# Where the weight sums of the last feed-forward stand: three of sixteen steps moved out of the recurrence's and the attention's parts

## The chip, the cores and the metric

The kernel runs on one core of a Trainium2 chip. A core has a matrix engine (TensorE, PE in the profile, with its weight loads as PEld), a vector engine (VectorE, DVE), a scalar engine (ScalarE, ACT), a general engine (GpSimd, POOL), and a queue engine that here issues transfers only (SyncE, SP). Each engine executes its own instructions strictly in order; semaphores order them between engines. Sixteen DMA engines, shared by all queues, move data between the main memory and SBUF. The metric is the device time of one execution in microseconds.

## The reference

One residual block of a streaming encoder, on x of 256 rows and 1024 columns in fp32: a half-weight SwiGLU feed-forward; a mixer with two branches; a cross attention to a memory of 256 rows; a second SwiGLU feed-forward.

```python
h = rmsnorm(x, ffn1_pre_g);  x = x + 0.5 * rmsnorm(swiglu(h, ffn1_w_in, ffn1_w_down), ffn1_post_g)
h = rmsnorm(x, mix_pre_g)
q_a, f_a, i_a, g_a, q_b, k_b, v_b, f_b, gates = split(h @ w_in)
o_a = rmsnorm(hgrn2_chunkwise(q_a, f_a, i_a, lb), hg_norm_g) * silu(g_a)   # gated linear recurrence, 8 heads of 128
o_b = fox_attention(q_b, k_b, v_b, f_b + fox_f_bias)                       # causal softmax with summed log forget gates
gate = sigmoid(gates + b_gate)
y = gate[0] * (o_a @ w_branch_a) + gate[1] * (o_b @ w_branch_b)
x = x + rmsnorm(y @ w_out, mix_post_g)
x = x + rmsnorm(mem_cross_attention(rmsnorm(x), rmsnorm(mem), w_mq, w_mkv, w_mo), mem_post_g)   # 4 heads of 256
h = rmsnorm(x, ffn2_pre_g);  x = x + 0.5 * rmsnorm(swiglu(h, ffn2_w_in, ffn2_w_down), ffn2_post_g)
```

## The kernel before

**Products.** Every large product is made to nearly fp32 accuracy from fp32r parts: an operand is split into a high part `hi` and a rest `lo`, and three matmuls (hi by hT, lo by hT, hi by lT) stand for one. Weights come from the main memory in pieces of 512 KB (`raw`, four buffers, issued on SP, L136). ACT casts a piece to `hi` (L137), DVE subtracts to get `lo` (L138); `hi` and `lo` have eight buffers each. A chunk of a projection is four pieces. Activations are split in the same way (`hT` by ACT, `lT` by DVE: L156 and L157, L271 and L272 with a gain, L1240 and L1241 for the memory's values). PSUM has buffers `mm` (2), `tr` (2) and `acc` (4). A product group of a projection that has its features on the partitions is 48 matmuls 256 wide into one `mm`. All matmuls go through one helper (L93); the scores of the attention and the inner products of the recurrence are plain fp32.

**Stages in order of time.** Feed-forward 1; the mixer's projections: input (`i_a`), forget gates (`f_a`, whose last products DVE takes up at 235 us), queries (`q_a`), output gates and forget logits; then the k and q of the attention (`k_b`, `q_b`), among which the recurrence is laid in pieces; from 345 us the attention with the values' projection (`v_b`), into which the transposes of the recurrence's output are laid (to 380); the branch gates (`gates`), the branches, `w_out`; the memory stage (`mk`, `mq`, `mv`), whose softmax is transposed at 565; feed-forward 2.

**The steps.** Feed-forward 2 computes four pairs of its chunks (3, 5, 7, 9: `QUADS_2`) with fewer products, from sums of weights. These sums are made beforehand, in 16 steps spread over the program. A step is `at(name, c)`: if `(name, c)` stands in the table `SUMS_AT`, four additions run on DVE over a 1 MB tile `wide` (L771 to L774, 128x512 each), then two transfers on POOL's queue write the result to the main memory (`sums<-wide`, L776), then `load_step()` loads the data of a later step by two transfers on POOL's queue (`wide<-in_wts_dram`, L759). The place of the call in the program, and `issue_after` the last DVE instruction recorded, set where the additions stand on DVE. Step number k in the table takes the k-th slot of weights; so when an entry is taken out, all later entries change their slot.

`wide` has two buffers: the load for step k+2 goes into the buffer of step k, so it waits until the writes of step k have landed. POOL's queue is in order: while its first instruction waits, everything behind it waits too, the masks of the attention among it. Up to the branch gates only `TO_GATES` slots are loaded, since one buffer of `wide` is then lent to the gates' bias (`brow`, L1115).

**The attention's start.** `cbc` and `cbm` are the summed log forget gates, spread over the partitions by transfers on POOL's queue (L1017, L1021); on `cbm` POOL lays the causal mask (`affine_select`, L1023). `cc` is transposed into a `tr` buffer and copied to `ct` by DVE (L1030). Two groups of diagonal scores go into `tr` buffers, two wide groups into `acc` buffers; these hold the recurrence's last sums until DVE has multiplied them into `G` (L1013), for which the reciprocal root `rstd` is worked out by a chain of one-column operations on DVE (`v`, `y`, `t`: L223 to L239). Then `G` is transposed by PE (L315) and split into `hT` and `lT`.

**The memory's softmax.** Scores in `acc`; row maxima on DVE (L1258), exponentials on ACT (L1262), division on DVE (`pm`, L1264), transposes on PE (L1268).

**What sets the order.** The program is recorded with a few numbers that place parts behind a given matmul (`after`); a scheduler then lays each engine's instructions out. So a step taken out can change the order of its neighbours.

Of the kernel before, what the change touches and what calls it, by code (L numbers as in the profile page):

```python
# [53 lines left out]
L_MX = 30  # L54

SUMS_AT = (
    ("i_a", 1), ("f_a", 0), ("f_a", 1), ("q_a", 0), ("k_b", 1), ("v_b", 1), ("gates", 1), ("gates", 3),
    ("br_a", 0), ("br_b", 0), ("br_a", 1), ("br_b", 1), ("mk", 1), ("mk", 3), ("mq", 1), ("mv", 1),
)
TO_GATES = 6  # L60
L_LAST = 12

_ORDER = [
# [15 lines left out]
def block_kernel(ctx: ExitStack, tc: tile.TileContext, wts, head_in, gf_in, x_in, mem_in, memT_in, cols, rows, fbias, masks, out):  # L79
# [23 lines left out]
    def nm(s):  # L103
        count[0] += 1
        return f"{s}_{count[0]}"

    def m4(shape, dt=F32, n="m"):
        return mp.tile(shape, dt, tag="m4", name=nm(n))
# [38 lines left out]
    def chunk(name, c):  # L147
        return [unit(name, 4 * c + i) for i in range(4)]
# [46 lines left out]
    def proj_col2(X, units, cbs):  # L195
        ps = mm()
        for j, cb in enumerate(cbs):
            proj_col(ps[:, j * T : (j + 1) * T], X, units, cb)
        return ps.rearrange("p (c t) -> p c t", c=2)

    def bc(a, shape, dim):
        return a.unsqueeze(dim).to_broadcast(shape)
# [546 lines left out]
    def load_step():  # L749
        if len(slots) < len(steps) and (brows or len(slots) < TO_GATES):  # L750
            c, q, i = steps[len(slots)]
            W = wp.tile([P, 2, 2, 512], F32, tag="wide", name=nm("wide"), bufs=2)
            for e in range(2):
                part, src = W[:, e].rearrange("p j n -> p (j n)"), wts[_AT["f2_in"] + 4 * (c + e - 1) + 2 * q + i]
                if len(slots) < 2:
                    with tc.issue_after(loads[-1]):
                        nc.sync.dma_start(part, src)
                else:
                    G.dma_start(part, src)  # L759
            slots.append(W)  # L760

    def at(name, c=0):

        if (name, c) not in SUMS_AT:
            return
        k = SUMS_AT.index((name, c))
        (u, q, i), W = steps[k], slots[k]
        last = next(x for x in reversed(nc.cur_bb.bb.instructions) if x.engine == mybir.EngineType.DVE)
        t1, t4, t3, t2 = (W[:, a, b] for a in range(2) for b in range(2))
        with tc.issue_after(last):  # L770
            V.tensor_tensor(out=t1, in0=t1, in1=t3, op=ALU.add)  # L771
            V.tensor_tensor(out=t3, in0=t3, in1=t2, op=ALU.add)
            V.tensor_tensor(out=t2, in0=t1, in1=t2, op=ALU.add)  # L773
            V.tensor_tensor(out=t4, in0=t2, in1=t4, op=ALU.add)  # L774
        for e in range(2):
            G.dma_start(sums[u][2 * e : 2 * e + 2, q, :, i * 512 : i * 512 + 512].rearrange("k p n -> p k n"), W[:, e])  # L776
        load_step()
# [33 lines left out]
    for c in range(2):  # L811
        u = chunk("f_a", c)
        f, k = m4([P, 4, T], n="f"), m4([P, 4, T], n="k")
        for j in range(2):
            js = slice(2 * j, 2 * j + 2)
            ps = proj_col2(X2, u, (2 * j, 2 * j + 1))
            f_last = V.tensor_tensor(out=f[:, js], in0=ps, in1=bc(row2, [P, 2, T], 1), op=ALU.mult).ins
            S.activation(f[:, js], f[:, js], AF.Sigmoid)
            for i in (2 * j, 2 * j + 1):
                hd = 4 * c + i  # L820
                V.tensor_scalar(out=f[:, i], in0=f[:, i], scalar1=olb[:, hd : hd + 1], scalar2=lbv[:, hd : hd + 1], op0=ALU.mult, op1=ALU.add)
        V.tensor_scalar(out=k, in0=f, scalar1=-1.0, scalar2=1.0, op0=ALU.mult, op1=ALU.add)
        fT.append(f)
        kT_.append(k)
        at("f_a", c)
    for c in range(2):
        u = chunk("q_a", c)
        q = m4([P, 4, T], n="q")
        for j in range(2):
            js = slice(2 * j, 2 * j + 2)  # L830
            ps = proj_col2(X2, u, (2 * j, 2 * j + 1))
            z = sp.tile([P, 2, T], F32, tag="z2", name=nm("z2"), bufs=3)
            V.tensor_tensor(out=z, in0=ps, in1=bc(row2, [P, 2, T], 1), op=ALU.mult)
            S.activation(q[:, js], z, AF.Sigmoid)
            V.tensor_tensor(out=q[:, js], in0=q[:, js], in1=z, op=ALU.mult)
        qT_.append(q)
        at("q_a", c)

# [133 lines left out]
    for c in range(2):  # L974
        for name, lst, sc in (("k_b", kb_, 1.0), ("q_b", qb_, 1.0 / math.sqrt(128.0))):
            u = chunk(name, c)
            t = m4([P, 4, T], n=name)
            m = len(log)
            for j in range(2):
                ps = proj_col2(X2, u, (2 * j, 2 * j + 1))  # L980
                for i in range(2):
                    V.scalar_tensor_tensor(out=t[:, 2 * j + i], in0=ps[:, i], scalar=sc, in1=row2, op0=ALU.mult, op1=ALU.mult)
            lst.append(t)
            at(name, c)
            if c == 0 and name == "k_b":
                forget(m + 30)

# [107 lines left out]
    for c in range(2):  # L1095
        u = chunk("v_b", c)
        t = m4([P, 2, 512], n="v_b")
        for h in range(2):
            ps = mm()
            proj_tok(ps, X2, u, h)  # L1100
            S.activation(t[:, h, :], ps, AF.Copy, scale=r2[h])
        vb_.append(t)
        at("v_b", c)
    for h in range(2):
        with after(len(log) - L_OA * (2 - h)):
            to_T(OA, lambda kb: Gt[h][:, kb * P : (kb + 1) * P], h, G_HG)
# [89 lines left out]
    for h in range(2):  # L1196
        rows_proj(po[h], Y, "w_out", h, range(0, 4))
        if h == 0:
            y_T(1, 1, m + L_Y)
    at("w_out", 0)  # L1200
    rowm = row_of(rm)
    rows_proj(po[0], Y, "w_out", 0, range(4, 8))
    post(po[0], 0, g2)
# [69 lines left out]
    def mem_out(i):  # L1273
        ps = trp()
        for j in range(2):
            o = ps[:, j * T : (j + 1) * T]
            for sb in range(2):

                n = sb * 512 + (2 * (i % 2) + j) * P
                vh = VM.h[i // 2][:, n // T, n % T : n % T + P]  # L1280
                vl = VM.l[i // 2][:, n // T, n % T : n % T + P]
                MM(o, vh, pT.h[sb][:, i], start=(sb == 0), stop=False)
                MM(o, vl, pT.h[sb][:, i], start=False, stop=False)
                MM(o, vh, pT.l[sb][:, i], start=False, stop=(sb == 1))
        i2 = slice(2 * (i % 2), 2 * (i % 2) + 2)
        split(AO.h[i // 2][:, i2], AO.l[i // 2][:, i2], ps.rearrange("p (a t) -> p a t", a=2))

    at("mv", 0)
    m = len(log)
    mem_v(1)  # L1290
    at("mv", 1)
# [2 lines left out]
            mem_out(i)  # L1294
    for i in range(2, 4):
        mem_out(i)
    X4 = Pair()
    r4 = [None, None]
    po = [[acc(), acc()], [acc(), acc()]]
# [7 lines left out]
    rows_proj(po[1], AO, "mo", 1, range(3, KB))  # L1307
    half(X4, r4, 0, G_F2, m + L_MO)
    post(po[1], 1, g3)


    def second(m):
        half(X4, r4, 1, G_F2, m + L_F2)

    ffn("f2_in", "f2_dn", X4, r4, 2, 3, QUADS_2, sums, None, second)

# [84 lines left out]
```

## Time and profile before

| | us |
|---|---|
| median of 3 runs (lowest, highest) | 789.82 (789.19, 791.26) |
| the profiled execution | 789.21 |
| its span on the core | 787.1 |
| PE busy in it | 775.7 (99%) |
| VectorE, ScalarE, GpSimd busy | 646.0, 469.5, 48.6 |

A row of an engine's timeline reads: start in us from the span's begin, duration in us, engine, line of the kernel, operation, output <- inputs, shapes, and xN for N like instructions in a row; in brackets the time for which the engine stood idle just before and what ended it. Matmuls are pipelined, so that the distance of their starts says more than their durations. "Chain" rows (the chain of work that ended last) have start, length, and the work or the wait. A fp32 product by PE shows as two records.

### The profile page before, as it was taken

The page shows a single profiled execution, that of the slowest core. Times are in us where ns is not written, and L with a number is a line of the kernel's source. Part 1 is how long each engine was busy: PE and PEld are TensorE (multiplying, and loading weights), DVE is VectorE, ACT ScalarE, POOL GpSimd, SP SyncE. Part 2 cuts the span into 40 slices and gives each one's busy share as a digit, 9 for nine tenths or more (in the row PEclk, how much of TensorE's full clock was granted, in tenths as well). Part 3 has the DMA queues.
Part 4 walks back from the last instruction along what each step waited for, and adds up shares of the span by engine and source line. Part 5 has one row for each costly group of instructions (what it writes and reads, how often), then busy time and mean ns, then how long its engine had stood idle before and what let it go on. Part 6 is the DMA issues. An engine that isn't in the chain of part 4 may idle for free.

```text
span 787.1 us, 13170 instructions
## 1 busy us (share of the span) xinstructions
PE 775.7 (99%) x5004; PEld 670.5 (85%) x5004; DVE 646.0 (82%) x1004; ACT 469.5 (60%) x704; POOL 48.6 (6%) x81
## 2 busy tenths in 40 slices
PE   9999999999999999999999999999999999999996
PEld 7888888887899999988788888999888888888884
DVE  6789989968788898689677886997777989888864
ACT  7665664756753447347675434745655758777753
POOL 0000000000102100030001221011000000000000
PEclk9999999999999999999999999999999999999998
DMA  9794484476679855584589999679664279889831
GB/s 346 247 311 159 160 294 148 160 248 244 252 258 311 277 189 162 178 293 132 192 286 327 376 355 359 210 259 334 231 200 148 84 262 374 315 312 344 321 126 54
DMA packets 57392, 193.61 MB, mean 246 GB/s; under 512 B 6249, under 2 KB 9713, under 8 KB 57329
## 3 DMA queue, kind: packets, MB, share of 16 engines
q1 hardware_dynamic: 48080, 159.60, 58.0%
q0 software_dynamic: 9104, 33.04, 12.0%
q8 instruction: 39, 0.64, 0.3%
q14 instruction: 25, 0.20, 0.1%
q10 hardware_dynamic: 144, 0.13, 0.0%
HBM read 174.92 MB, written 17.83 MB: 245 GB/s over the span
## 4 chain that ended last, share of the span: by engine, by line
PE 96%; DVE 1%; DMA 1%; ACT 1%; issue 1%; DVEq 0%; ACTq 0%
PE mm L93 62%; PE acc L93 27%; PE tr L93 4%; PE tr L395 1%; DMA raw<-in_wts_dram 1%; PE tr L315 1%; PE tr L1069 0%; ACT hi L137 0%; PE tr L1161 0%; PE tr L1268 0%; DVE lo L138 0%; ACT L357 0%; DVE y L229 0%; DVE t L227 0%; PE tr L406 0%
## 5 line engine op out<-in xcount | busy, mean ns | idle before, releaser
L138 DVE TENSOR_TENSOR lo<-raw,hi 128x1024 fp32r<-128x1024 f32 (+1 forms) x228 | 270.3, 1201 | 59.6 <-ACT hi L137 55.7
L137 ACT CAST hi<-raw 128x1024 fp32r<-128x1024 f32 (+1 forms) x228 | 232.4, 1036 | 120.5 <-PE mm L93 69.6
L93 PE MATMUL mm<-lo,hT 128*128 128x512 f32 (+1 forms) x448 | 171.2, 386 | 0.0
L93 PE MATMUL mm<-hi,hT 128*128 128x512 f32 (+1 forms) x448 | 170.7, 385 | 0.0
L93 PE MATMUL mm<-hi,lT 128*128 128x512 f32 (+1 forms) x448 | 170.6, 385 | 0.0
L93 PE MATMUL acc<-hi,act 128*128 128x512 f32 x352 | 113.2, 391 | 0.0
L93 PE MATMUL mm<-hT,hi 128*128 128x256 f32 x384 | 109.1, 284 | 0.1
L93 PE MATMUL mm<-hT,lo 128*128 128x256 f32 x384 | 109.0, 284 | 0.0
L93 PE MATMUL mm<-lT,hi 128*128 128x256 f32 x384 | 108.9, 284 | 0.0
L93 PEld LDWEIGHTS mm<-hi,hT 128*128 128x128 f32 x448 | 84.2, 188 | 16.1 <-ACT hT L271 0.7
L93 PEld LDWEIGHTS mm<-hi,lT 128*128 128x128 f32 x448 | 84.1, 188 | 15.8 <-DVE lT L272 0.5
L93 PEld LDWEIGHTS mm<-lo,hT 128*128 128x128 f32 x448 | 84.0, 188 | 14.8
L93 PEld LDWEIGHTS acc<-hi,act 128*128 128x128 f32 x352 | 65.9, 188 | 13.7 <-DVE act L157 0.2
L93 PEld LDWEIGHTS mm<-hT,hi 128*128 128x128 f32 x384 | 73.6, 192 | 0.5 <-issue 0.3
L93 PEld LDWEIGHTS mm<-hT,lo 128*128 128x128 f32 x384 | 73.6, 192 | 0.1
L93 PEld LDWEIGHTS mm<-lT,hi 128*128 128x128 f32 x384 | 73.6, 192 | 0.1
L93 PE MATMUL acc<-lo,act 128*128 128x512 f32 x176 | 69.0, 392 | 0.0
L157 DVE TENSOR_TENSOR lo<-wide,hi 128x1024 fp32r<-128x1024 f32 x40 | 48.0, 1219 | 2.0 <-ACT hi L156 1.4
L156 ACT CAST hi<-wide 128x1024 fp32r<-128x1024 f32 x40 | 41.5, 1051 | 12.3 <-DVE wide L494 7.5
L776 POOL DMA_DIRECT2D sums<-wide x32 | 23.6, 738 | 394.8 <-DVE wide L773 238.1
L93 PEld LDWEIGHTS acc<-lo,act 128*128 128x128 f32 x176 | 33.1, 188 | 6.7
L93 PE MATMUL mm<-hi,sh 128*128 128x512 f32 x96 | 37.5, 390 | 0.0
(243 smaller groups left out, 1130.2 us busy)
## 6 DMA issues: line engine op xcount, KB each, us to landing
raw<-in_wts_dram SPq DMA_DIRECT2D x232, 512.0 KB, 5.2
sums<-wide POOLq DMA_DIRECT2D x32, 512.0 KB, 5.8
wide<-sums SPq DMA_DIRECT2D x32, 512.0 KB, 6.8
wide<-in_wts_dram POOLq DMA_DIRECT2D x28, 512.0 KB, 6.6
wide<-in_wts_dram SPq DMA_DIRECT2D x12, 512.0 KB, 6.3
raw<-in_gf_dram SPq DMA_DIRECT2D x12, 344.0 KB, 4.7
head<-in_head_dram SPq DMA_DIRECT2D x8, 388.0 KB, 6.2
grow<-in_rows_dram SPq DMA_DIRECT2D x4, 512.0 KB, 6.9
```

Source lines behind the costliest of these rows:

```text
L93: log.append(PE.matmul(*args, **kw).ins)
L137: S.copy(h, r)
L138: V.tensor_tensor(out=l, in0=r, in1=h.bitcast(F32), op=ALU.subtract)
L156: S.copy(hi, src)
L157: V.tensor_tensor(out=lo, in0=src, in1=hi.bitcast(F32), op=ALU.subtract)
L315: PE.transpose(ps[:, j * P : (j + 1) * P], src(kb), ident)
L395: PE.transpose(trv[:, j, h * P : (h + 1) * P], ats[c, h][:, j * P : (j + 1) * P], ident)
L776: G.dma_start(sums[u][2 * e : 2 * e + 2, q, :, i * 512 : i * 512 + 512].rearrange("k p n -> p k n"), W[:, e])
```

## The change

Three steps leave their places (behind the first query chunk of the recurrence `q_a` 0, the second key and query chunk `k_b` 1, the second value chunk `v_b` 1). The call among the forget gates moves into the inner loop, so there are four places instead of two there; the table names three of them. The entries `mq` 0 (behind the memory's first query chunk) and `ao` 0 (a new call behind the memory's outputs) are new. `TO_GATES` goes from 6 to 4: two slots fewer are loaded ahead of the branch gates. Calls that no entry names any more are taken out.

```diff
 SUMS_AT = (
-    ("i_a", 1), ("f_a", 0), ("f_a", 1), ("q_a", 0), ("k_b", 1), ("v_b", 1), ("gates", 1), ("gates", 3),
-    ("br_a", 0), ("br_b", 0), ("br_a", 1), ("br_b", 1), ("mk", 1), ("mk", 3), ("mq", 1), ("mv", 1),
+    ("i_a", 1), ("f_a", 0), ("f_a", 2), ("f_a", 3), ("gates", 1), ("gates", 3), ("br_a", 0), ("br_b", 0),
+    ("br_a", 1), ("br_b", 1), ("mk", 1), ("mk", 3), ("mq", 0), ("mq", 1), ("mv", 1), ("ao", 0),
 )
-TO_GATES = 6
+TO_GATES = 4
...
@@ -819,10 +819,10 @@
             for i in (2 * j, 2 * j + 1):
                 hd = 4 * c + i
                 V.tensor_scalar(out=f[:, i], in0=f[:, i], scalar1=olb[:, hd : hd + 1], scalar2=lbv[:, hd : hd + 1], op0=ALU.mult, op1=ALU.add)
+            at("f_a", 2 * c + j)
         V.tensor_scalar(out=k, in0=f, scalar1=-1.0, scalar2=1.0, op0=ALU.mult, op1=ALU.add)
         fT.append(f)
         kT_.append(k)
-        at("f_a", c)
...
-        at("q_a", c)
...
-            at(name, c)
...
-        at("v_b", c)
...
-    at("w_out", 0)
...
-    at("mv", 0)
...
     for i in range(2, 4):
         mem_out(i)
+    at("ao", 0)
```

VectorE at the attention's start, before. The rows of lines 771 to 773 are additions of the step behind `v_b` 1; `ct` is the copy that frees a `tr` buffer.

```order
L223 TENSOR_SCALAR v_3901<-ss_666_3898 128x1
L138 TENSOR_TENSOR lo_4158<-raw_4156,hi_4157 128x1024
L225 TENSOR_SCALAR y_3903<-v_3901 128x1
L771 TENSOR_TENSOR wide_2432<-wide_2432 128x512
L227 TENSOR_SCALAR t_3905<-v_3901,y_3903 128x1
L772 TENSOR_TENSOR wide_2432<-wide_2432 128x512
L229 TENSOR_SCALAR y_3907<-t_3905,y_3903 128x1
L1030 COPY ct_3970<-tr_3971 128x16
L231 TENSOR_SCALAR t_3909<-v_3901,y_3907 128x1
L773 TENSOR_TENSOR wide_2432<-wide_2432 128x512
```

The same place now (the lines have moved up by two):

```order
L223 TENSOR_SCALAR v_3889<-ss_664_3886 128x1
L138 TENSOR_TENSOR lo_4146<-raw_4144,hi_4145 128x1024
L225 TENSOR_SCALAR y_3891<-v_3889 128x1
L227 TENSOR_SCALAR t_3893<-v_3889,y_3891 128x1
L229 TENSOR_SCALAR y_3895<-t_3893,y_3891 128x1
L231 TENSOR_SCALAR t_3897<-v_3889,y_3895 128x1
L233 TENSOR_SCALAR t_3899<-t_3897 128x1
L235 TENSOR_SCALAR y_3901<-t_3899,y_3895 128x1
L239 TENSOR_SCALAR rstd_3903<-y_3901 128x1
L1028 COPY ct_3958<-tr_3959 128x16
L1011 TENSOR_SCALAR G_2568<-acc_3876,rstd_3903,G_2568 128x512
L1011 TENSOR_SCALAR G_2568<-acc_3877,rstd_3903,G_2568 128x512
```

The additions are gone, the whole chain to `rstd` stands ahead of `ct`, and the two `G` follow `ct` at once.

TensorE at the same place, before. `tr` with `k_b,q_b` are diagonal scores, `acc` with `k_b,q_b` wide scores, `mm` is the values' projection.

```order
L1029 MATMUL tr_3971<-ident,cc 128x8 x2
L93 MATMUL tr_3975<-k_b_2848,q_b_2985 128x128 x4
L93 MATMUL tr_4018<-k_b_3112,q_b_3245 128x128 x4
L93 MATMUL mm_4086<-hi_4062,hT_1700 128x512
L93 MATMUL mm_4086<-lo_4063,hT_1700 128x512
L93 MATMUL mm_4086<-hi_4062,lT_1701 128x512
L93 MATMUL mm_4086<-hi_4062,hT_1700 128x512
L93 MATMUL mm_4086<-lo_4063,hT_1700 128x512
L93 MATMUL acc_3994<-k_b_2848,q_b_2985 128x256 x2
L93 MATMUL acc_3995<-k_b_2848,q_b_2985 128x256 x2
```

And now:

```order
L1027 MATMUL tr_3959<-ident,cc 128x8 x2
L93 MATMUL tr_3963<-k_b_2842,q_b_2979 128x128 x4
L93 MATMUL tr_4006<-k_b_3106,q_b_3233 128x128
L93 MATMUL acc_3982<-k_b_2842,q_b_2979 128x256 x2
L93 MATMUL acc_3983<-k_b_2842,q_b_2979 128x256 x2
L93 MATMUL tr_4006<-k_b_3106,q_b_3233 128x128 x3
L93 MATMUL mm_4074<-hi_4050,hT_1700 128x512
L93 MATMUL mm_4074<-lo_4051,hT_1700 128x512
```

The first wide scores moved ahead of the projection, between the first and the other three diagonal scores of the second group.

GpSimd from the spreading of `cbc` to the first branch gates, before:

```order
L1017 DMA cbc_3958<-cd 128x8x128
L776 DMA sums_1773<-wide_2292 128x2x512 x2
L1021 DMA cbm_3960<-cd 128x1024
L1021 DMA cbm_3965<-cd 128x1024
L1023 AFFINE_SELECT cbm_3960<-cbm_3960 128x1024
L1023 AFFINE_SELECT cbm_3965<-cbm_3965 128x1024
L776 DMA sums_1773<-wide_2432 128x2x512 x2
L759 DMA wide_4352<-in_wts_dram 128x1024 x2
```

And now:

```order
L1015 DMA cbc_3946<-cd 128x8x128
L1019 DMA cbm_3948<-cd 128x1024
L1019 DMA cbm_3953<-cd 128x1024
L1021 AFFINE_SELECT cbm_3948<-cbm_3948 128x1024
L1021 AFFINE_SELECT cbm_3953<-cbm_3953 128x1024
L759 DMA wide_4334<-in_wts_dram 128x1024 x2
```

The writes of two steps no longer stand between the loads of the masks and the load for the step in the branch gates.

VectorE in the memory stage, around the second half of the memory's first query chunk (`mq` 0; `lT` with `mm` is its split), before:

```order
L138 TENSOR_TENSOR lo_5979<-raw_5977,hi_5978 128x1024
L138 TENSOR_TENSOR lo_5985<-raw_5983,hi_5984 128x1024
L157 TENSOR_TENSOR lT_5734<-mm_5786,hT_5733 128x512
L138 TENSOR_TENSOR lo_5991<-raw_5989,hi_5990 128x1024
L157 TENSOR_TENSOR lT_5862<-mm_5863,hT_5861 128x512
L138 TENSOR_TENSOR lo_6175<-raw_6173,hi_6174 128x1024
```

And now:

```order
L138 TENSOR_TENSOR lo_5973<-raw_5971,hi_5972 128x1024
L138 TENSOR_TENSOR lo_5979<-raw_5977,hi_5978 128x1024
L157 TENSOR_TENSOR lT_5716<-mm_5768,hT_5715 128x512
L771 TENSOR_TENSOR wide_5502<-wide_5502 128x512
L138 TENSOR_TENSOR lo_5985<-raw_5983,hi_5984 128x1024
L772 TENSOR_TENSOR wide_5502<-wide_5502 128x512
L773 TENSOR_TENSOR wide_5502<-wide_5502 128x512
L774 TENSOR_TENSOR wide_5502<-wide_5502 128x512
L157 TENSOR_TENSOR lT_5853<-mm_5854,hT_5852 128x512
L138 TENSOR_TENSOR lo_6169<-raw_6167,hi_6168 128x1024
```

Four additions stand between the two splits, and behind them the order is that of before. The slots have moved on by two: the step that follows at `mq` 1 uses the slot whose load stood for `mv` 1.

## The prediction

> **What bounds the kernel now.** I read the page's busy times first, then the waits of TensorE (PE) alone, the page's table of transfers (the last number is the median of us from issue to landing), then the places where PE waits, and last the stages that receive the moved steps.
>
> ```profile
> PE   775.7 (99%) x5004; PEld 670.5 (85%) x5004; DVE 646.0 (82%) x1004; ACT 469.5 (60%) x704; POOL 48.6 (6%) x81
> ...
> PE tr L93 <- DVE ct L1030: 1.0, 1, 1.0
> PE tr L315 <- DVE lT L272: 0.9, 1, 0.9
> ...
> raw<-in_wts_dram SPq DMA_DIRECT2D x232, 512.0 KB, 5.2
> sums<-wide POOLq DMA_DIRECT2D x32, 512.0 KB, 5.8
> ...
> wide<-in_wts_dram POOLq DMA_DIRECT2D x28, 512.0 KB, 6.6
> ```
>
> PE is busy 775.7 of 787.1 us. The change adds and removes no matmul, so it can gain only what PE waits, and lose only by making PE wait. Of its waits (us in total, times, longest) these two lie near a moved step: on `ct` and on a `lT`. They are what there is to win. The granted clock is 1.00 in all windows quoted below, so it explains nothing here.
>
> **Place 1: the start of the attention's scores (345 to 352 us).** PE, then DVE, then POOL:
>
> ```profile
> 345.43 1.16 PE L93 MATMUL tr<-k_b,q_b 128*128 128x128 f32 x8
> 347.58 1.16 PE L93 MATMUL tr<-k_b,q_b 128*128 128x128 f32 x8 [0.99 <-DVE ct L1030]
> 349.85 1.99 PE L93 MATMUL acc<-k_b,q_b 128*128 128x256 f32 x8
> 351.50 0.58 PE L93 MATMUL mm<-hi,lT 128*128 128x512 f32 x1
> ```
>
> ```profile
> 344.23 0.68 DVE L771 TENSOR_TENSOR wide<-wide 128x512 f32<-128x512 f32 x1
> 344.83 1.04 DVE L227 SCALAR_TENSOR_TENSOR t<-v,y 128x1 f32<-128x1 f32 x1
> 345.80 0.68 DVE L772 TENSOR_TENSOR wide<-wide 128x512 f32<-128x512 f32 x1
> 346.40 1.04 DVE L229 SCALAR_TENSOR_TENSOR y<-t,y 128x1 f32<-128x1 f32 x1
> 347.36 0.16 DVE L1030 COPY ct<-tr 128x16 f32<-128x16 f32 x1
> 347.47 0.22 DVE L231 SCALAR_TENSOR_TENSOR t<-v,y 128x1 f32<-128x1 f32 x1
> ...
> 349.05 1.40 DVE L1013 SCALAR_TENSOR_TENSOR G<-acc,rstd,G 128x512 f32<-128x512 f32 x2
> ```
>
> ```profile
> 335.62 1.46 POOL L776 DMA_DIRECT2D sums<-wide  x2 [31.73 <-DVE wide L774]
> 337.08 1.12 POOL L1021 DMA_DIRECT2D cbm<-cd  x2
> 344.69 2.74 POOL L1023 TENSOR_SCALAR_AFFINE_SELECT cbm<-cbm 128x1024 f32<-128x1024 f32 x2 [6.49 <-DMA cbm<-cd]
> 368.62 1.11 POOL L759 DMA_DIRECT2D wide<-in_wts_dram  x2 [3.66 <-DMA sums<-wide]
> ```
>
> The copy `ct` frees the PSUM buffer that PE's second group of score products needs. Two additions of step 5 (L771, L772) stand ahead of it on DVE, and so do two one-column operations that took 1.04 us each, where the like operation at 347.47 took 0.22. Those two lie inside the 2.74 us of POOL's AFFINE_SELECTs; the masks' loads (`cbm`, L1021) had started late because on POOL they stood behind step 4's writes, which waited 31.73 us for DVE. So both removed steps feed this wait.
>
> What it is worth: from 345.43 to 351.50 pass 6.07 us. The chain of waits has an undisturbed piece for the transposing records (and, behind it, the links of place 2):
>
> ```profile
> 365.45 0.87 PE tr L315 x8
> ...
> 370.35 7.18 DMA raw<-in_wts_dram
> 377.55 1.05 ACT hi L137
> ...
> 379.16 0.62 DVE lT L272 x2
> ```
>
> Sixteen such records cost 2 x 0.87, the eight `acc` records 1.65 (349.85 to 351.50), and the five 512-wide matmuls between them 5 x 0.23 (the step from 378.28 to 378.51 in place 2 below): 4.54. The excess is 1.53: the wait of 0.99, and about 0.5 for switching between the fp32 scores and the fp32r projection. After the change the row order has the first four `acc` scores right behind the first `tr`, ahead of the projection, which takes out one of the switches; and DVE has nothing but short operations before `ct`. Without the additions (1.2 us) and the slow pair (1.6 us over normal), the chain from `y` to `rstd` is done by about 345.2, `ct` by 345.6 (PE's transposes of `cc` stand right ahead of the row at 345.43), and the two `G` (1.40) by 347.0. PE needs `ct` at 345.43 + 0.87 = 346.30, the first `G` at 346.5 and the second at 347.4: no wait beyond 0.1. I take a gain of 1.3 us; the bounds are 0.8 (half of the old wait comes back on `G`, and the switches still cost 0.2) and 1.53.
>
> [...]
>
> **Place 2: the transposes of the recurrence's output (370 to 380 us).**
>
> ```profile
> 376.19 0.39 PE L93 MATMUL mm<-hi,lT 128*128 128x512 f32 x1
> 376.63 0.66 PE L315 MATMUL tr<-ident,G 128*128 128x128 f32 x4
> ...
> 378.28 0.40 PE L93 MATMUL mm<-hi,lT 128*128 128x512 f32 x1
> 378.51 0.39 PE L93 MATMUL mm<-hi,hT 128*128 128x512 f32 x1
> 379.82 0.66 PE L315 MATMUL tr<-ident,G 128*128 128x128 f32 x4 [0.92 <-DVE lT L272]
> ```
>
> Matmuls follow at 0.23 (378.28 to 378.51), but 376.19 to 376.63 is 0.44 and 378.51 to 379.82 is 1.31: 0.21 + 1.08 lost. The chain above names the cause: `lT` and `hT` stand behind a weight cast (ACT L137) that waited for its raw weights, a transfer of 7.18 us against the median of 5.2. In the same microseconds POOL loads 1 MB (368.62) for the step after the attention, and the transfer engines are full:
>
> ```profile
> 235.00:260.00 25.00, 25.00 (x214) 24.78 (x216) 22.97 (x36) 9.64 (x14) 6.03 (x11) 1.00 0.90 301
> ...
> 370.00:380.00 10.00, 9.03 (x43) 6.91 (x42) 7.74 (x15) 7.99 (x16) 0.00 (x0) 1.00 1.01 360
> ...
> 545.00:550.00 5.00, 5.00 (x23) 4.13 (x22) 5.00 (x7) 2.13 (x3) 0.00 (x0) 1.00 0.96 327
> ...
> 560.00:600.00 40.00, 39.91 (x213) 34.09 (x212) 25.83 (x42) 20.93 (x40) 1.45 (x2) 1.00 0.46 154
> ```
>
> (Columns: window, its length, busy us of PE, PE's weight loads, DVE, ACT and POOL, clock, DMA share, GB/s.) In the new order that load follows the AFFINE_SELECTs directly, near 330, and no step's data is awaited in between; its 1.05 MB at 360 GB/s are 2.9 us of transfer that leave this window, where the raw weights were late by 0.5 to 2. DVE also reaches these weights some 2 us sooner. I take 1.2 of the 1.29; the bounds are 0 (the order on ACT alone makes the wait) and 1.29.
>
> **The forget gates' stage (211 to 257 us).** It holds steps 2 and 3 now, with step 4 just behind; afterwards it holds all three, each four additions (0.68 us), two writes and, but for the last two, two loads. PE lost nothing there (25.00 of 25.00) with DVE at 22.97 of 25. What could fail is that the last of the three steps waits for its slot, which is loaded once the writes of the first have landed. Three product groups of 48 matmuls lie between them, at 25.00 / 214 = 0.117 us each 16.8 us; the additions (4 x 0.68), a write (5.8) and a load (6.6) with 1.1 of issue take 16.2. So it just fits. Cost 0; the bound is 1.0, a slot late by 1.6 less that 0.6 of margin, all of it on PE.
>
> **The memory stage (540 to 595 us).** The step after the first query chunk is new; so 2 MB more (its writes, and the load that they release) and 2.4 us of DVE come into the fullest stretch.
>
> ```profile
> 542.04 1.11 POOL L759 DMA_DIRECT2D wide<-in_wts_dram  x2 [8.77 <-DMA sums<-wide]
> ...
> 543.82 3.50 DVE L138 TENSOR_TENSOR lo<-raw,hi 128x1024 fp32r<-128x1024 f32 x3 [3.22 <-ACT hi L137]
> ...
> 547.84 0.68 DVE L771 TENSOR_TENSOR wide<-wide 128x512 f32<-128x512 f32 x1
> ...
> 562.80 1.22 DVE L1264 TENSOR_TENSOR pm<-pm,sm 128x1024 f32<-128x1024 f32 x1
> ...
> 565.55 1.03 PE L1268 MATMUL tr<-ident,pm 128*128 128x128 f32 x8
> ```
>
> The additions fit into the 3.22 us that DVE waits before 543.82. The step at 547.84 now uses the slot whose load is issued at 542.04; the two transfers need 6.6 from 542.6, so DVE waits until about 549.1, 1.3 us. What PE needs first behind that is `pm`, done at 564.02 and used at 565.55: a slack of 1.5. So 0 if the raw weights come as before. In bulk 2.1 MB at 360 GB/s are 5.8 us: if they all went ahead of the weights, 5.8 - 1.5 = 4.3 would reach PE, and with the 1.3 added 5.6. The nearest row is the 7.18 us transfer of place 2, where 1 MB of the same kind made a weight 2.0 us later than the median; against a slack of 1.5 that is 0.5 here if that weight is among those that DVE splits ahead of `pm`, and 0 if not. I take 0, since PE takes those weights up some chunks later and only DVE's order ties them to `pm`.
>
> The last step, behind the memory outputs, falls into 560 to 600, with DVE at 25.83 of 40 and DMA at 0.46: 2.4 us of additions there are hidden. If they were not, DVE's delay of 2.4 would reach PE in full. The additions, loads and writes are as many as before (16 steps), so nothing else is removed.
>
> **Sum.** 1.3 + 1.2 - 0 - 0 = 2.5 us from the profiled execution's 789.2 (span 787.1 and 2.1 around it): 786.7. The median of the runs, 789.82, lies 0.6 above that execution, so I forecast 787.3, 0.32% less.
>
> **The rivals.**
>
> 1. One wait stays. If place 2's wait is made by ACT's own order and not by the crowded transfers, or `G` takes over from `ct`, only one gain comes: 789.82 - 1.3 = 788.5. For it: `G` comes two rows behind `ct`, and 0.1 to 0.2 of its slack is all there is. Against it: the chain shows DMA, not ACT, ahead of the cast.
>
> 2. Slower: the memory stage's softmax is late. The mechanism is the 2 MB shared out with the raw weights in 545 to 560, where DMA starts from 0.96 busy. It decides once `pm` is later than 1.5 us; it turns the sign at 1.5 + 2.5 = 4.0 us, and the full 5.6 give 789.82 - 2.5 + 5.6 = 792.9. Against it: DMA has 0.46 from 560 on, so the surplus can run off there. [...]
>
> 3. The AFFINE_SELECTs block DVE where they go (about 320 to 330): at most 2.74 us there, against this DVE row:
>
> ```profile
> 327.28 2.36 DVE L138 TENSOR_TENSOR lo<-raw,hi 128x1024 fp32r<-128x1024 f32 x2 [3.85 <-ACT hi L137]
> ```
>
> An idle time of 3.85 takes 2.74 in, so this gives no other time; if it stood on the busy stretch behind, 1 us would be the cost and 788.3 the time.
>
> **Chances.** 0.3% is 2.4 us, about what a measurement of this kernel can tell from no change: faster is below 787.45, slower above 792.2. Both waits go: 0.62, between 786.3 and 788.3, and 0.46 of it lies below 787.45, the rest within. Rival 1: 0.14; rival 2 by halves 0.08 and rival 3 or a late step among the forget gates 0.03, all within. Rival 2 in bulk: 0.13, above. So faster 0.46, same 0.41, slower 0.13. The range runs from 785.6 (both gains at their upper bounds, 2.8, and the lowest run as far below the median as before, 0.6, with 0.8 more) to 791.2, which leaves out most of the bulk case; the likeliest case alone is 786.3 to 788.3.
>
> **What would show it.** In the new profile the waits of PE on `ct` and on `lT` (L272) are gone, the AFFINE_SELECT row starts before 331 and no 1.04 us row of one column stands beside it, POOL's load at 368 is at about 330, and the window 370 to 380 has DMA under 1. DVE's L771 near 548 shows a wait of about 1.3 on its load. Wrong I would be by a new wait of PE on `G`, or on `pm` at L1268 in the memory stage, or by raw transfers over 7 us at 545 to 560.

## The result, and the profile after

The changed kernel takes 785.06 us (median of 4 runs, 784.41 to 785.18) against 789.88 (4 runs, 789.19 to 791.26): a ratio of 0.9935, interval 0.9918 to 0.9952. A second set gave 785.35 against 789.80, ratio 0.9949 (0.9936 to 0.9962). It is faster by 4.5 to 4.8 us. The forecast was 787.3, so the sign was right, the gain was about twice the 2.5 us that I had summed, and the time lies below my range.

The profiled execution of the changed kernel took 785.17 (span 783.4). The page's busy times, and behind them the whole list of what PE still waits for:

```profile
PE 774.3 (99%) x5004; PEld 669.9 (86%) x5004; DVE 646.2 (82%) x1004; ACT 468.4 (60%) x704; POOL 48.4 (6%) x81
...
raw<-in_wts_dram SPq DMA_DIRECT2D x232, 512.0 KB, 5.1
```

```profile
PE tr L93 <- DVE ones L206: 1.1, 1, 1.1
```

Both waits that I set out to win, on `ct` and on `lT`, are gone. What is left is the one at the start. But those two waits were the 2.5 us of my sum, and the gain is 4.5. To see where the rest lies I cut PE's timeline at five instructions that every version has: the first decayed product of the recurrence, the transposes of `cc` before the scores, the first transposes of the output `G`, those of `p` in the branch gates, and those of `pm` in the memory stage. Before:

```profile
259.90 1.44 PE L93 MATMUL acc<-q,k 128*32 128x32 f32 x128
...
345.21 0.28 PE L1029 MATMUL tr<-ident,cc 8*128 8x8 f32 x2
...
365.29 1.03 PE L315 MATMUL tr<-ident,G 128*128 128x128 f32 x8
...
389.13 0.60 PE L1069 MATMUL tr<-ident,p 128*128 128x128 f32 x4
```

And after:

```profile
259.06 1.46 PE L93 MATMUL acc<-q,k 128*32 128x32 f32 x128
...
343.97 0.28 PE L1027 MATMUL tr<-ident,cc 8*128 8x8 f32 x2
...
362.79 1.03 PE L315 MATMUL tr<-ident,G 128*128 128x128 f32 x8
...
385.23 0.60 PE L1067 MATMUL tr<-ident,p 128*128 128x128 f32 x4
...
561.57 1.03 PE L1264 MATMUL tr<-ident,pm 128*128 128x128 f32 x8
```

The differences of these starts, with the same cuts through the profiled executions of the experiments below (us; the span's end closes the last column):

| kernel | start to first product | recurrence | place 1 | place 2 | branch gates to memory | to the end |
|---|---|---|---|---|---|---|
| before | 259.90 | 85.31 | 20.08 | 23.84 | 176.42 | 221.55 |
| changed | 259.06 | 84.91 | 18.82 | 22.44 | 176.34 | 221.83 |
| changed, again | 259.58 | 84.79 | 18.61 | 22.43 | 176.32 | 221.57 |
| values' step back | 259.73 | 86.48 | 18.56 | 23.60 | 176.35 | 221.48 |
| keys' step back | 260.03 | 88.19 | 20.01 | 22.42 | 176.38 | 221.57 |
| 260 us load late | 259.84 | 85.07 | 20.08 | 23.94 | 176.35 | 221.52 |
| masks early | 260.12 | 85.95 | 18.53 | 24.11 | 176.28 | 221.61 |
| gates' load late | 259.80 | 86.16 | 19.99 | 22.43 | 177.60 | 221.52 |
| these three together | 259.46 | 84.91 | 18.54 | 22.42 | 176.50 | 221.47 |
| memory step at `mv` 0 | 259.24 | 84.71 | 18.52 | 22.44 | 176.36 | 222.63 |
| 260 us load put back | 259.50 | 85.73 | 18.53 | 22.44 | 176.35 | 221.85 |

Place 1 gave 1.26 (1.47 in experiment 1) and place 2 gave 1.40. The recurrence, where I had expected nothing, gave 0.4 to 0.5 in these executions. The first column varies by over a microsecond, and all of that arises in the first 14 us, where every version issues the same work: PE's 51st record starts between 13.02 us (changed) and 14.07 (masks early), at 13.83 before, and from it to the first decayed product pass 246.0 to 246.1 us in ten of the eleven profiles (246.4 with the keys' step back). So the 0.84 that this column adds to the first pair is no work of the change.

The rows of place 1 after the change, PE, then DVE, then POOL:

```profile
344.18 1.38 PE L93 MATMUL tr<-k_b,q_b 128*128 128x128 f32 x10
345.60 1.99 PE L93 MATMUL acc<-k_b,q_b 128*128 128x256 f32 x8
347.43 0.83 PE L93 MATMUL tr<-k_b,q_b 128*128 128x128 f32 x6
348.02 0.47 PE L93 MATMUL mm<-hi,hT 128*128 128x512 f32 x1
```

```profile
343.52 0.22 DVE L227 SCALAR_TENSOR_TENSOR t<-v,y 128x1 f32<-128x1 f32 x1
...
344.68 0.16 DVE L1028 COPY ct<-tr 128x16 f32<-128x16 f32 x1
344.80 1.41 DVE L1011 SCALAR_TENSOR_TENSOR G<-acc,rstd,G 128x512 f32<-128x512 f32 x2
```

```profile
323.15 1.09 POOL L1021 TENSOR_SCALAR_AFFINE_SELECT cbm<-cbm 128x1024 f32<-128x1024 f32 x1 [5.74 <-DMA cbm<-cd]
326.74 1.47 POOL L1021 TENSOR_SCALAR_AFFINE_SELECT cbm<-cbm 128x1024 f32<-128x1024 f32 x1 [2.50 <-DMA cbm<-cd]
328.16 1.06 POOL L759 DMA_DIRECT2D wide<-in_wts_dram  x2
```

The masks are finished at 328.2 instead of 347.4, the one-column operation takes 0.22 instead of 1.04, `ct` stands at 344.68, and the load for the branch gates' step is issued at 328.16 instead of 368.62. In place 2 PE runs through, with the transfer engines at 0.67 where they stood at 1.01:

```profile
367.00:377.00 10.00, 10.00 (x49) 8.16 (x48) 7.56 (x14) 8.07 (x17) 0.00 (x0) 1.00 0.67 231
```

### The profile page after: what moved, and what is told of

It reads as the page before. It is cut to its first block, busy times and chain, and to the rows that moved or that the text cites. A ratio compares the mean times of both kernels' runs of the same rounds, so it can differ in the third digit from the quotient of the medians.

```text
span 783.4 us, 13175 instructions
## 1 busy us (share of the span) xinstructions
PE 774.3 (99%) x5004; PEld 669.9 (86%) x5004; DVE 646.2 (82%) x1004; ACT 468.4 (60%) x704; POOL 48.4 (6%) x81
## 4 chain that ended last, share of the span: by engine, by line
PE 99%; ACT 0%; DVE 0%; issue 0%; DVEq 0%; ACTq 0%
PE mm L93 64%; PE acc L93 28%; PE tr L93 4%; PE tr L395 1%; PE tr L315 1%; PE tr L1067 0%; PE tr L1158 0%; PE tr L1264 0%; ACT L357 0%; PE tr L406 0%; DVEq L1393 0%; DVE xs L376 0%; ACT hT L156 0%; ACT y L357 0%; ACT junk L243 0%
```

## The experiments

Every version here computes the whole reference output; none leaves work out.

### 1. The changed kernel once more

> The changed kernel once more, timed in turns with the kernel before. In the two profiled executions the gain is 1.2 us at the attention's start, 1.4 at the transposes of the recurrence's output, 0.5 in the recurrence near 268 us, and 0.8 within the first 10 us, where both kernels issue the same work. Theory A: the part in the first 10 us is chance, so more runs give 3.1 to 4.0 us less than before, and a second profile has the first product at another time. Theory B: it belongs to the change, and the difference stays 4.8.

Measured: 785.35, ratio 0.9949 (0.9936 to 0.9962), and the table's third row. The two places repeat, and of the 0.84 before the first product 0.32 is left. So the first pair's difference there was in good part chance. The medians differ by 4.45, between the two theories: more than the 4.0 that theory A allows, and more than the two places hold.

### 2. One step back: the values', without the keys'

From the changed kernel:

```diff
-    ("i_a", 1), ("f_a", 0), ("f_a", 2), ("f_a", 3), ("gates", 1), ...
-    ("br_a", 1), ("br_b", 1), ("mk", 1), ("mk", 3), ("mq", 0), ("mq", 1), ("mv", 1), ("ao", 0),
+    ("i_a", 1), ("f_a", 0), ("f_a", 2), ("f_a", 3), ("v_b", 1), ("gates", 1), ...
+    ("br_a", 1), ("br_b", 1), ("mk", 1), ("mk", 3), ("mq", 1), ("mv", 1), ("ao", 0),
-TO_GATES = 4
+TO_GATES = 5
...
+        at("v_b", c)
```

This puts two of the step's additions back ahead of `ct`, while the masks stay early on POOL. The step at `mq` 0 is left out for it.

> The changed kernel with the step behind the second value chunk put back (the one behind the first query chunk of the memory left out for it). Additions stand ahead of the copy ct again and the load for the branch gates' step is behind them again, near 366 us; the masks stay early. Theory A: ct is 1.2 us later than in the changed kernel, so PE waits 0.5 to 0.8 there and has the old order of scores, 1.2 lost in all; the transposes wait again, 1.2 to 1.4 lost: 787.6. Rival (the slow pair of one-column operations beside AFFINE_SELECT made the whole wait on ct): 0.4 lost at the first place, 786.7.

Measured: 789.32, ratio 0.9996 (0.9986 to 1.0006): the whole gain is gone. But place 1 is not where it went: 18.56, as short as in the changed kernel, with two additions in front of `ct` (345.23 and 345.96, `ct` at 346.63). Both theories missed the time. The cuts show two other losses. Place 2 is back at 23.60, because the branch gates' load again waits for the values' writes. And the recurrence starts late, at a wait of PE that neither of the two kernels has. POOL, DVE and PE of this version:

```profile
241.48 1.11 POOL L759 DMA_DIRECT2D wide<-in_wts_dram  x2 [5.81 <-DMA sums<-wide]
```

```profile
254.31 0.88 DVE L138 TENSOR_TENSOR lo<-raw,hi 128x688 fp32r<-128x688 f32 x1 [6.95 <-ACT hi L137]
```

```profile
262.48 0.46 PE L93 MATMUL acc<-q,k 128*32 128x32 f32 x32 [1.59 <-DVE q L835]
```

With `TO_GATES` at 5 a third load goes out among the forget gates, with the last writes (1.46 us of issue at 242.59) right behind it. A raw weight comes late (ACT waits 8.23 us for its transfer ahead of the cast at 253.51), DVE idles 6.95 us ahead of its split, and `q` is late for PE by 1.59. In the changed kernel that row is shorter by four microseconds of idle time:

```profile
249.33 0.88 DVE L138 TENSOR_TENSOR lo<-raw,hi 128x688 fp32r<-128x688 f32 x1 [2.92 <-ACT hi L137]
```

So one load more, with three steps in this stage, is what it cannot take: the wait on `q` stands in both profiles that have this load (here and in experiment 3) and in no other. With three steps here, `TO_GATES` at 4 is what keeps it out. The two losses make 2.8 us in this profile, which lies 1.0 under the median of its runs; that 1.0 is not placed.

### 3. The other step back: the keys', without the values'

As experiment 2, with `("k_b", 1)` in place of `("v_b", 1)`. Now POOL's masks again stand behind a step's writes, and no addition stands ahead of `ct`.

> The changed kernel with the step behind the second key chunk put back (the one behind the first query chunk of the memory left out for it). The masks' loads and AFFINE_SELECTs are late again; no addition stands ahead of ct; the load for the branch gates' step follows the AFFINE_SELECTs near 346 us. Theory A: two one-column operations of 1.0 us stand ahead of ct again, PE waits about 1.0, and the transposes near 375 wait for nothing: 786.1. Rival (the additions made the wait on ct): 785.1, as the changed kernel.

Measured: 788.95, ratio 0.9987 (0.9979 to 0.9996); both theories missed the time, since neither had the wait on `q`. Place 1 is at 20.01, as long as before, though the additions aren't there. PE, DVE and POOL of this version:

```profile
350.32 0.49 PE L93 MATMUL tr<-k_b,q_b 128*128 128x128 f32 x2 [0.73 <-DVE ct L1029]
```

```profile
347.62 0.97 DVE L229 SCALAR_TENSOR_TENSOR y<-t,y 128x1 f32<-128x1 f32 x1
...
348.87 0.93 DVE L233 SCALAR_TENSOR_TENSOR t<-t 128x1 f32<-128x1 f32 x1
```

```profile
347.49 2.31 POOL L1022 TENSOR_SCALAR_AFFINE_SELECT cbm<-cbm 128x1024 f32<-128x1024 f32 x2 [6.31 <-DMA cbm<-cd]
```

The one-column operations are slow again (0.93 and 0.97) inside the AFFINE_SELECTs. With experiment 2 this settles place 1: late masks alone make it, and the additions make none of it. Place 2 is short here (22.42), as the branch gates' load no longer waits for a step of the values. The recurrence lost as in experiment 2, by a wait of 1.65 on `q`, and in this execution, the slowest of its eleven, the granted clock fell too (last section).

### 4. From the kernel before: the load at 260 us put off

What had vanished in the recurrence besides additions was a load: before, POOL issued 1 MB at 259.71, at the first product. Here, in the kernel before, that load alone waits for the first keys and goes out at 302.40:

```diff
+            if late and len(slots) == 5:
+                V.tensor_copy(W[:, 0, 0, 0:1], late[0][:, 3, 0:1])
+                V.tensor_copy(W[:, 1, 0, 0:1], late[0][:, 3, 0:1])
...
-        load_step()
+        if (name, c) != ("q_a", 0):
+            load_step()
...
+                late.append(t)
+                load_step()
```

> The kernel before, with the 1 MB load that POOL issues at 259.7 us put off to about 300 us (it waits for the first keys of the attention). Theory A: the wait of PE without a releaser near 268 us came from this load, which crowds the transfers there; it goes, with 0.4 to 0.6 us: 789.3. Rival: the wait near 268 us has nothing to do with transfers: it stays, 789.9.

Measured: 788.51, ratio 0.9986 (0.9978 to 0.9995): 1.3 us less than the 789.80 beside it. In the profiled execution the recurrence is only 0.24 shorter; there the wait without a releaser near 268 us is gone, and one of 0.26 stands at 289.81. Place 2 stands as before. Place 1 is as long as before, but PE waits there on `G` (0.87) instead of `ct`: here an AFFINE_SELECT met an addition, which took 1.58 us instead of 0.68.

```profile
346.41 1.58 DVE L777 TENSOR_TENSOR wide<-wide 128x512 f32<-128x512 f32 x1
```

So this load cost something that appears in the runs, and less in the one profile of before.

### 5. From the kernel before: the masks ahead of the writes

The keys' writes are held back on POOL behind the masks' loads (in the trace one write goes out at 336.47, between these loads and the AFFINE_SELECTs, the other behind them); every addition stays where it was.

```diff
+        if name == "k_b":
+            held.append((u, q, i, W))
+            return
...
+    for u, q, i, W in held:
+        for e in range(2):
+            G.dma_start(sums[u]..., W[:, e])
```

> The kernel before, all sixteen steps in their places; only the writes of the step behind the second key chunk are issued behind the masks' loads on POOL's queue, so that the AFFINE_SELECTs are done by about 338 us. The additions of the next step still stand ahead of ct. Theory A: the slow pair of one-column operations made the wait on ct; it goes, with 1.3 to 1.5 us: 788.4. Rival (the additions made it, as half of my sum had it): at most 0.5 less, 789.3.

Measured: 788.09, ratio 0.9984 (0.9971 to 0.9996), and place 1 at 18.53. Its DVE and POOL:

```profile
345.69 0.22 DVE L227 SCALAR_TENSOR_TENSOR t<-v,y 128x1 f32<-128x1 f32 x1
345.82 0.69 DVE L773 TENSOR_TENSOR wide<-wide 128x512 f32<-128x512 f32 x1
346.43 0.15 DVE L229 SCALAR_TENSOR_TENSOR y<-t,y 128x1 f32<-128x1 f32 x1
346.49 0.17 DVE L1038 COPY ct<-tr 128x16 f32<-128x16 f32 x1
```

```profile
337.26 2.13 POOL L1027 TENSOR_SCALAR_AFFINE_SELECT cbm<-cbm 128x1024 f32<-128x1024 f32 x2
```

The additions interleave with the chain as before, the one-column operations take 0.15 and 0.22, and place 1 has its full gain, in PE's old row order as well, so the change of order that I priced at some tenths was not needed either. With the masks late, one operation of DVE beside each of the two AFFINE_SELECTs was longer by 0.8 to 0.9 us in three traces: 1.04 and 1.04 against 0.22 and 0.15 before, 0.97 and 0.93 against 0.15 in experiment 3, 1.05 and 1.58 against 0.22 and 0.68 in experiment 4. The addition at 345.80 before lies inside the AFFINE_SELECTs too and took its 0.68; what makes an operation slow there is not shown. On PE the price was 1.5 us (20.01 against 18.56 in experiments 3 and 2, 20.08 against 18.53 before and here).

This execution also shows what the 260 us load does in a bad case. PE, in the recurrence's 128 small products:

```profile
266.93 1.16 PE L93 MATMUL acc<-q,k 128*32 128x16 f32 x113
269.27 0.31 PE L93 MATMUL acc<-q,k 128*32 128x16 f32 x15 [1.19 <-issue]
```

### 6. From the kernel before: the branch gates' load put off

Copies of one column make the load wait until the branch gates' first activations are done, so that nothing of POOL's is in place 2. It goes out at 397.30 instead of 368.62.

```diff
+            if len(slots) in late:
+                for e in range(2):
+                    V.tensor_copy(W[:, e, 0, 0:1], late[len(slots)])
...
+    late[6] = zs[0][:, 1, 0:1]
```

> The kernel before, with the 1 MB load at 368.6 us put off to about 398 us, behind the second product of the first gate chunk (it is first used at 409). Theory A: the raw weights near 375 come in time and the wait on lT goes, 1.2 to 1.4 us less: 788.4. Rival (the order on ACT makes that wait): 789.8, the wait stays.

Measured: 788.75, ratio 0.9989 (0.9973 to 1.0005). Place 2 is at 22.43, and PE is full there:

```profile
370.00:380.00 10.00, 10.00 (x49) 8.30 (x49) 9.15 (x16) 8.20 (x17) 0.00 (x0) 1.00 0.87 299
```

So POOL's 1 MB made the whole wait of place 2; ACT's own order made none of it: the column is 23.60 to 24.11 in the four profiles with the load there, and 22.42 to 22.44 in the seven without. The median fell by 1.0, and the interval holds 1. In this profile two other parts are longer than before. The recurrence has 0.85 more: PE stops without a releaser for 0.65 near 268 us and for 0.35 each at 275.49 and 290.86. The stretch from the branch gates to the memory has 1.2 more (177.60 against 176.42), between 423 and 511 us. That isn't the late load alone, since experiment 7 has it as late and takes 176.50; I have not found its cause.

### 7. All three edits in the kernel before

Experiments 4, 5 and 6 together: the additions of all sixteen steps at the places that they had before the change, and of the writes only the keys' held back.

> The kernel before with three edits together and no step moved: the masks early, the load at 259.7 put off to 300, the load at 368.6 put off to 398. Theory A: all of the gain came from these three, and the additions on DVE cost nothing: 0.6 + 1.4 + 1.4 = 3.4 less by the traces, 4.0 less by the medians: 785.8 to 786.4. Rival: the additions in the recurrence and the attention cost 1 us or more by themselves: 787 or more.

Measured: 785.50, ratio 0.9948 (0.9929 to 0.9967), the changed kernel's time, and its cuts agree with the changed kernel's to 0.4 us in every column. The start's wait is the only one left in its list of PE's waits. So the additions of the three moved steps had cost PE nothing that can be seen where they stood. The gain of the change is that of three things on POOL's queue: one load not beside the first products, the masks not behind a step's writes, and one load not beside the transposes of `G`. Alone they gave 1.3, 1.7 and 1.0 us in the medians, 4.0 of the 4.25 that they give together (the last of the three by itself is not clear of the noise).

### 8. The changed kernel with the memory step at another place

```diff
-    ..., ("mk", 3), ("mq", 0), ("mq", 1), ("mv", 1), ("ao", 0),
+    ..., ("mk", 3), ("mq", 1), ("mv", 0), ("mv", 1), ("ao", 0),
...
+    at("mv", 0)
```

> The changed kernel, with the step behind the memory's first query chunk put ahead of its second value chunk, where DVE idles. Theory A: the step in the fullest stretch of transfers costs nothing there: 785.2, as the changed kernel. Rival (raw weights are late and PE waits for pm at the softmax): 0.4 to 1.4 less, 784.0 to 784.8.

Measured: 786.01, ratio 0.9951 (0.9938 to 0.9965). The memory stage up to `pm` is the same (176.36); behind it PE has a new wait, and the last column is 1.1 longer than in experiment 1:

```profile
PE tr L315 <- DVE xs L342: 1.0, 1, 1.0
```

So the step at `mq` 0 took nothing ahead of `pm` that moving it gives back, and the other place is no better.

### 9. The changed kernel with the 260 us load put back

The converse of experiment 4: the next load may go out behind `q`, as it did before the change.

```diff
-        if len(slots) < len(steps) and (brows or len(slots) < TO_GATES):
+        if len(slots) < len(steps) and (brows or len(slots) < TO_GATES or (late and len(slots) == 4)):
...
+            if late and len(slots) == 4:
+                V.tensor_copy(W[:, 0, 0, 0:1], late[0][:, 3, 0:1])
+                V.tensor_copy(W[:, 1, 0, 0:1], late[0][:, 3, 0:1])
...
+        if c == 1:
+            late.append(q)
+            load_step()
```

> The changed kernel with one transfer put into the recurrence: the 1 MB load for the step in the branch gates is issued behind the last query product, near 258 us, instead of 328; it is needed at 406 in both. Theory A: the transfers crowd out the block of instructions that PE fetches near 262 to 266 us (queue 8); it comes after 265, and PE stops within the burst of 128 small products near 266 us for 0.4 to 1.2 us, with no releaser shown: 785.6 to 786.6. Rival: the stop came from something else of the kernel before (the later writes, the other order): no wait there, 785.2.

Measured: 786.44, ratio 0.9965 (0.9951 to 0.9978): 1.1 and 1.4 us over the two medians of the changed kernel. Experiment 1 ran on another chip; against the kernel before beside it (789.27) the gain is 2.8 where the changed kernel has 4.5 to 4.8, so by that the cost is 1.6 to 2.0. POOL and PE:

```profile
259.97 1.11 POOL L763 DMA_DIRECT2D wide<-in_wts_dram  x2 [15.68 <-DVE wide L756]
```

```profile
266.45 1.16 PE L93 MATMUL acc<-q,k 128*32 128x16 f32 x113
268.13 0.32 PE L93 MATMUL acc<-q,k 128*32 128x16 f32 x15 [0.52 <-issue]
```

The stop that experiment 5 showed comes back with the load, and of the cuts only the recurrence grows, by 0.8 to 0.9. Before had it too, at 0.41, and the changed kernel runs the same 128 products without a break:

```profile
266.83 1.16 PE L93 MATMUL acc<-q,k 128*32 128x16 f32 x113
268.40 0.31 PE L93 MATMUL acc<-q,k 128*32 128x16 f32 x15 [0.41 <-issue]
```

```profile
266.01 1.30 PE L93 MATMUL acc<-q,k 128*32 128x16 f32 x128
```

That the load makes this stop is shown, by taking it away (4 and 7) and by putting it back (9): all four profiles with the load have it, none of the seven without. Smaller losses there have no such load: in experiment 7 the row takes 1.58 us instead of 1.30, with the load 35 us behind it, and the stops of 0.26 to 0.35 at 275 to 291 us in experiments 4 and 6 have no transfer of POOL's near them.

```profile
266.26 1.58 PE L93 MATMUL acc<-q,k 128*32 128x16 f32 x128
```

## Why the prediction came out as it did

**The sum's missing term.** The step that failed is the reading of PE's waits: "Of its waits … these two lie near a moved step", and with it "so nothing else is removed". The list had a fourth row, behind those three that the start, `ct` and `lT` make:

```profile
PE acc L93 <- issue: 0.4, 1, 0.4
```

It is the stop of 0.41 at 268.40, 8.7 us behind a load that the change takes away from there; I passed it over since it names no engine. I had counted loads over the whole kernel, where they are as many, but not at the place that they left. Its size is 0.4 to 0.5 by the cuts of before against the changed kernel's, 0.8 to 1.2 by those of experiments 5 and 9, 1.3 in the medians of 4 (0.4 to 1.7 by the interval), and 1.1 to 2.0 in those of 9.

A second term of the sum failed with it: the 0.6 from before's profiled execution to its median, which I carried over as an even offset. The changed kernel has none, with 785.17 profiled against a median of 785.06, and 785.07 against 785.35. It may be that before's profile is one that the 260 us load had touched little, since it lost less there than experiments 5 and 9; no run shows that this was the 0.6.

**Place 1: the size right, the cause half wrong.** I took 1.3; it gave 1.26 and 1.47. But the working gave 1.2 us of the chain to the additions, and said that "both removed steps feed this wait". Experiments 2, 5 and 7 keep the additions and have the full gain; 3 takes them away and has none. In experiment 5 the second addition ends at 346.51 and `ct`, whose transposes start on PE at 346.07, runs at 346.49, so the additions filled time in which `ct` was not ready yet. Beside the AFFINE_SELECTs operations of 0.15 and 0.22 took 1.04 each, and that was the wait. The masks came early because the writes ahead of them on POOL were gone, as I had said.

**Place 2: right.** I took 1.2 of 1.29; it gave 1.40, a tenth over the bound. Experiment 6 rules out ACT's order, which was rival 1. Its other half, that `G` takes over from `ct`, happened in experiments 4 and 6, where the masks are late (0.87 and 0.76), and not in the changed kernel.

**The forget gates' stage: cost 0, right, and nearer the edge than I knew.** PE has no gap:

```profile
235.00:260.00 25.00, 25.00 (x302) 24.78 (x304) 20.25 (x32) 8.66 (x13) 2.03 (x5) 1.00 0.72 236
```

The wait on the last slot that I feared did not reach PE. (The 1.6 in its bound of 1.0 has no row behind it.) What would have failed is a load more (experiments 2 and 3: 1.6 to 1.7 us of PE).

**The memory stage: 0, right; the wait forecast on the way to it did not come.** POOL and DVE:

```profile
535.13 1.11 POOL L759 DMA_DIRECT2D wide<-in_wts_dram  x2 [6.19 <-DMA sums<-wide]
```

```profile
543.85 0.68 DVE L771 TENSOR_TENSOR wide<-wide 128x512 f32<-128x512 f32 x1
...
558.97 1.23 DVE L1260 TENSOR_TENSOR pm<-pm,sm 128x1024 f32<-128x1024 f32 x1
```

I had taken the load's issue from the old order, 5.8 us ahead of the step (by its own numbers the forecast wait is 1.4, not 1.3); it went out 8.7 ahead (535.13 to 543.85), since the writes that release it landed after 6.19 us of waiting, not 8.77. `pm` is done at 560.2 and used at 561.57, a slack of 1.4 as before (1.5). One sign that I had named for being wrong was there: the eight raw transfers issued from 541.1 to 555.5 took 7.6 us in the median (6.0 to 9.2), where those issued from 545.1 to 559.3 before took 5.3 (4.9 to 6.0). So the mechanism of rival 2 came, about 2.3 us on a weight, but its price didn't: `pm` kept its slack, PE has no wait there, and experiment 8 finds nothing hidden in it. The halves of this rival's smaller case in the chances are shown by no run; POOL's transfers (q0) and SP's (q1) shared the engines unevenly: 90% and 14% of their time from 373.5 to 374 us before, 34% and 66% from 375.5 to 376, and in the changed kernel 98% and 2% from 541 to 544, 2% and 99% from 545 to 549. Taking those weights to be needed only some chunks later was the step that held. Rival 3 was right in that it gives no other time: the recurrence did not grow.

**The range.** Both known gains at their upper bounds, a low execution and 0.8 more gave 785.6. The range had no room for a term that I had not seen, and the measured time lies 0.5 under it.

**What stays open.** In medians 4.5 to 4.8 went; places 1 and 2 hold 2.7 to 2.9 and the 260 us load 1.1 to 2.0. The rest, at most 1.0, is within the intervals, and I have not placed it.

## What to carry to other kernels

When a step is moved, follow its transfers rather than its arithmetic: ask of each place that it leaves which load, write or issue is gone from the queue there, and look at each wait of TensorE there, also the ones that name no other engine. Before pricing instructions on an engine's path by their durations, see whether neighbours run at their normal speed; the slow ones may be the whole wait. Where one profile lies under its kernel's median, don't carry the difference over to the changed kernel as it stands: here it was 0.6 before and gone after.

## What the runs showed of the hardware that I had not expected

**TensorE stopped within a burst of small products while a load filled the transfer engines.** A row of 128 products of 16 columns, each with its weight load (256 instructions in 1.3 us), shows no other engine that it waits for, yet stopped behind the 113th in the four profiles with the load. The transfers' share in the ten microseconds ahead of it, before and then after:

```profile
255.00:265.00 10.00, 10.00 (x187) 9.74 (x186) 8.73 (x12) 5.39 (x8) 1.11 (x2) 1.00 0.95 328
```

```profile
255.00:265.00 10.00, 10.00 (x186) 9.72 (x185) 9.23 (x13) 5.21 (x8) 0.00 (x0) 1.00 0.51 146
```

In the transfers by queue, cut in half-microseconds, one packet of q8, a queue to which the page gives the kind "instruction", falls into these microseconds: at 265.5 before, at 262.5 after. The program has 39 such packets, one for every 257 of PE's 2 x 5004 products and weight loads, and before they come at PE's pace: 7 from 260 to 297 us beside 1920 records of PE and PEld, 6 from 591 to 761 us beside 1549, or 274 and 258 records to a packet. So I take q8 to be PE's. It comes at 265.5 or 266.5 in all four profiles with the stop (before, 5, 6, 9), and at 262.5 to 264.5 in those without (after, 1, 2, 4, 7, 8; in experiment 3 the clock fell there, and it is left aside). My estimate from these times is that in the stop PE waits for the instructions of this packet, which is late beside the load's packets. The times fit, loads or not: the later the packet starts, the more PE loses in the row. In experiment 5 it starts with the first of the 128 products, and the row with its stop lasts 1.4 us longer than in the changed kernel. With 0.7 us of lead (6) that is 0.8, with 0.8 (9) 0.7, with 0.9 (before) 0.6, and with 1.6 (7, without the load) 0.3; with 2.5 us or more it is nothing. That is argued all the same: no run moved this packet alone. PE's idle time in the four profiles with the load was 0.41 to 1.19 us.

**The granted clock fell once behind a short stop.** In experiment 3 the granted clock fell after the wait on `q` (1.7 us) at the start of the recurrence:

```profile
260.00:265.00 5.00, 3.35 (x139) 3.15 (x139) 5.00 (x7) 1.22 (x3) 0.00 (x0) 0.94 0.68 211
265.00:270.00 5.00, 5.00 (x25) 5.00 (x24) 4.16 (x7) 2.62 (x4) 0.00 (x0) 0.71 0.51 141
```

Experiment 2, with a wait of 1.59 at the same place, kept 1.00. Its recurrence took 86.48 against 88.19, so the fall cost up to 1.7 us in that execution. Whether the wait set it off is not shown: of the kernel before, whose profile has no such wait, the three longest executions beside experiments 5 to 8 (792.19 to 793.61) have a mean clock of 0.995 to 0.996, where the other 26 have 0.997 or more.
